# A decoder layer's two feed-forwards: the chunk pairs that take seven products, the engine that sums x, and the place of the raw weights

## The chip, the cores and the metric

The kernel runs on one core of one Trainium2 chip. The metric is the device time of one execution in microseconds (us); the lower the better. The core's engines run side by side, each through its own instructions in order: TensorE (PE in the profile; PEld is its loading of the stationary operand), VectorE (DVE), ScalarE (ACT), GpSimd (POOL) and SyncE (SP), which here does nothing but issue transfers. They wait for one another through semaphores.

## The reference, cut to what matters

One layer works on 256 tokens of width 2048 in float32: a feed-forward, a mixer (windowed attention beside an RWKV-7 recurrence), a cross-attention into 256 memory tokens, a second feed-forward, and a last norm. The change touches the two feed-forwards alone, whose inner width is 5632.

```python
def rms_norm(x, g):
    xf = x.astype(jnp.float32)
    y = xf * lax.rsqrt(jnp.mean(xf * xf, axis=-1, keepdims=True) + NORM_EPS)
    return (y * g.astype(jnp.float32)).astype(x.dtype)

def swiglu(h, w_gate, w_up, w_down):
    return (jax.nn.silu(h @ w_gate) * (h @ w_up)) @ w_down
...
x = x + 0.5 * swiglu(rms_norm(x, ffn1_norm[l]), ffn1_w_gate[l], ffn1_w_up[l], ffn1_w_down[l])
x = gated_parallel_mixer(...)
x = memory_cross_attention(...)
x = x + 0.5 * swiglu(rms_norm(x, ffn2_norm[l]), ffn2_w_gate[l], ffn2_w_up[l], ffn2_w_down[l])
return rms_norm(x, final_norm)
```

## The kernel before, in words

**Stages.** Three pools of on-chip memory follow one another: f1 holds the first feed-forward (0 to about 740 us in the profiled execution), mx the mixer and the cross-attention (to about 1570 us), f2 the second feed-forward (to the end). Pools f2 and mx use the same addresses; a tile of f2 waits for those tiles of mx that lay where it lies. At the end of the cross-attention GpSimd writes x to memory (x3d); in f2 `reload` (L1360, a transfer on GpSimd's queue for each of four column blocks) brings it back as the residual to which the feed-forward adds.

**Products.** A matmul of float32 is made of three of a rounded type (`times`, L397 to 399): with x = xhi + xlo and a weight = hi + lo, they are xhi by hi, xhi by lo, xlo by hi. Each handles 128 tokens, a chunk of 128 of the summed dimension, and 512 output columns.

**Weights.** A unit is two chunks by 512 columns of raw weights. SyncE loads them (`load`, L301 to 316) 4 items ahead, 8 in a feed-forward: there mostly two units together, in a tile raw2 (4 buffers) of the current pool, else one, in a tile raw (4 buffers). `split_unit` makes hi on ScalarE (L324) and lo = raw - hi on VectorE (L325), `AHEAD` = 2 units before TensorE wants them. `next_item` calls both.

**One feed-forward.** The 11 blocks of 512 inner columns go in `GROUPS` of 4, 4 and 3; after each group comes its part of the down product (L621 adds it to x). The first block of all makes gate and up by plain `product`, 12 matmuls a unit. Every other block makes both together in `product_pair`: eight chunk pairs q of two chunks each, as 2 x 2 blocks (two token halves by two chunks on one side, two chunks by gate and up on the other). In most pairs that is eight products of three matmuls, 24 in all. In the pairs of `SEVEN` it is seven products, p1 to p7, 21 matmuls, in the manner of Strassen and Winograd. They need sums of x's blocks and sums of the weights. The p-values lie in PSUM banks: p1, p3 and p5 in the three banks mm, p2 and p4 in acc (three banks), p6 and p7 in tr (two banks, which the transposes use as well). After the last pair of `SEVEN`, ScalarE copies p1 to the tile hb, and VectorE combines p5, p6, p7 and hb to the tiles u2, u3 (L499 to 501). The later pairs run plainly on p2 to p5. At the last of them (q = 7) VectorE adds the rest (L513, 516, 520), ScalarE applies Silu (L514, 517), and VectorE multiplies gate and up (L521) into hb.

**Sums of the weights** (`sums`, L328 to 344), for every block and every pair in `SEVEN`: four additions (L335 to 338) on VectorE, two casts to thi on ScalarE (L340), two tlo = sum - thi on VectorE (L341).

**Sums of x** (`combinations`, L409 to 446), once in a feed-forward. For each pair q up to the last in `SEVEN`, GpSimd adds xhi and xlo to one float32 tile (L423), and makes from it four sums (a pair in `SEVEN`, L429 to 432) or two differences (a pair before the last of `SEVEN` that is not in it: `EARLY`, L435). Then ScalarE casts them to chi (L438), and VectorE forms clo (L440). The tiles u between them have two buffers. In the code a pair's sums start once its x chunks are made (`x.done`).

**x and its norm.** `Norm.block` transposes x by blocks (`feat`), and ScalarE casts it to xhi (L560), VectorE makes xlo (L561), and ScalarE squares it for the norm (L569). After the fourth block `rstd` (L576 to 583) makes the scale r of each token: VectorE reduces the squares' sums, GpSimd takes the power -1/2 (L582). The scale is applied behind the gate and up products, so x goes unscaled into the matmuls. The Silu of the first block (L607) is the first that reads r.

**Transposes of hb.** `transposed` brings a finished block's hb to the layout of the down product: two `feat` (four transposes each into a bank tr, L534), each followed by `split` (a cast to hhi on ScalarE, L537; hlo on VectorE).

**Order.** Sums of x, transposes, reloads and the like are Python generators in groups (`Interleave`); the products call `tick`, and each tick lets every group go one step. The framework then orders each engine's instructions anew within what the data allow, and puts the semaphores.

Of the kernel before, what the change touches and what calls it, by code (L numbers as in the profile page):

```python
# [34 lines left out]
AHEAD, LOADED = 2, 4  # L35


SEVEN = (1, 3)
EARLY = tuple(q for q in range(max(SEVEN)) if q not in SEVEN)


# [87 lines left out]
def decoder_layer(ctx: ExitStack, tc: tile.TileContext, a: dict, out: bass.AP):  # L129
# [276 lines left out]
                k + i == 0, k + i == nk - 1,  # L406
            )

    def combinations(sp, x: Act):  # L409


        n = 4 * len(SEVEN) + 2 * len(EARLY)
        parts = [sp.tile([P, n, P], F32R, tag="c" + e, name="c" + e) for e in ("hi", "lo")]
        c = {"parts": parts, "at": {}, "done": False}

        def work():
            o = 0
            for q in range(max(SEVEN) + 1):
                while not {2 * q, 2 * q + 1} <= x.done:
                    yield  # L420
                v = sp.tile([P, 2, 2, P], F32, tag="u", name="u", bufs=2)
                f = sp.tile([P, 4, P], F32, tag="u", name="u", bufs=2)
                pool.tensor_tensor(  # L423
                    v[:].rearrange("p k t n -> p k (t n)"), f32(x.at(0, 2 * q, 2)),
                    f32(x.at(1, 2 * q, 2)), ALU.add,
                )
                if q in SEVEN:
                    n = 4
                    pool.tensor_tensor(f[:, 0], v[:, 0, 1], v[:, 1, 1], ALU.add)  # L429
                    pool.tensor_tensor(f[:, 1], f[:, 0], v[:, 0, 0], ALU.subtract)  # L430
                    pool.tensor_tensor(f[:, 2], v[:, 0, 0], v[:, 0, 1], ALU.subtract)
                    pool.tensor_tensor(f[:, 3], v[:, 1, 0], f[:, 1], ALU.subtract)
                else:
                    n = 2
                    pool.tensor_tensor(f[:, :2], v[:, :, 0], v[:, :, 1], ALU.subtract)  # L435
                yield from idle(3)
                s = slice(o, o + n)
                act.copy(parts[0][:, s], f[:, :n])  # L438
                dve.tensor_tensor(parts[1][:, s], f[:, :n], f32(parts[0][:, s]), ALU.subtract)
                c["at"][q] = o  # L440
                o += n
                yield
            c["done"] = True

        bg.spawn("mem", work())
        return c

    def product_pair(sp, x: Act, c, r, w):

        pw, _, nk, _, n = plan[at["product"]]
        assert pw[0].tensor is w.tensor
        at["product"] += 1
        b, begun = {}, set()
        hb = sp.tile([P, 2, 512], F32, tag="hb", name="hb", bufs=2)
        u2, u3 = (sp.tile([P, 512], F32, tag="u", name="u", bufs=2) for _ in range(2))
        late = nk // KU - 1  # L460

        def add(to, x_, w_, last):
            if to not in b:
                b[to] = {"p1": mm, "p3": mm, "p5": mm, "p2": acc, "p4": acc}.get(to, tr)()
            times(
                b[to][:], x_, w_, to not in begun, last, skip_group_check=True,
            )
            begun.add(to)

        def of_x(t, k):  # L470
            return [x.at(p, k)[:, t * P : (t + 1) * P] for p in range(2)]

        def of_c(q, i):
            return [p[:, c["at"][q] + i, :] for p in c["parts"]]

        def of_w(parts_, i):
            return [p[:, i, :] for p in parts_]

        for q in range(nk // KU):
            k = KU * q  # L480
            last = q == late
            if q in SEVEN:
                bg.until(lambda: c["done"])
                g, u, s = next_item()
                end = q == max(SEVEN)
                seven = (
                    ("p1", of_x(0, k), of_w(g, 0), end), ("p2", of_x(0, k + 1), of_w(g, 1), False),
                    ("p3", of_c(q, 3), of_w(u, 1), False), ("p5", of_c(q, 0), of_w(s, 0), end),
                    ("p7", of_c(q, 2), of_w(s, 1), end), ("p6", of_c(q, 1), of_w(s, 2), end),
                    ("p4", of_x(1, k + 1), of_w(s, 3), False),  # L490
                )
                for i, p in enumerate(seven):
                    add(*p)
                    if i % 2:
                        bg.tick()
                    if end and i == 1:
                        act.copy(hb[:, 0], b["p1"][:])
                if end:
                    dve.tensor_tensor(u2[:], b["p6"][:], hb[:, 0], ALU.add)  # L499
                    dve.tensor_tensor(u3[:], b["p7"][:], u2[:], ALU.add)  # L500
                    dve.tensor_tensor(u2[:], b["p5"][:], u2[:], ALU.add)
                continue
            g, u = next_item()
            for to, t, wt in (("p2", 0, g), ("p4", 1, g), ("p3", 0, u), ("p5", 1, u)):
                for i in range(KU):
                    off = to == "p3" and q in EARLY
                    add(
                        to, of_c(q, i) if off else of_x(t, k + i), of_w(wt, i),
                        last and i == KU - 1,
                    )  # L510
                if last:
                    if to == "p2":
                        dve.tensor_tensor(hb[:, 0], b["p2"][:], hb[:, 0], ALU.add)  # L513
                        act.activation(hb[:, 0], hb[:, 0], AF.Silu, scale=r[0])  # L514
                    elif to == "p4":
                        dve.tensor_tensor(hb[:, 1], b["p4"][:], u3[:], ALU.add)
                        act.activation(hb[:, 1], hb[:, 1], AF.Silu, scale=r[1])
                    else:
                        t, v = (0, u2) if to == "p3" else (1, u3)
                        dve.tensor_tensor(v[:], b[to][:], v[:], ALU.add)  # L520
                        dve.scalar_tensor_tensor(  # L521
                            hb[:, t], v[:], r[t], hb[:, t], ALU.mult, ALU.mult
                        )
                bg.tick()
        return hb
# [18 lines left out]
    class Norm:  # L544
        def __init__(self, gain, x=None):
            self.gain = gain
            self.ss = stat.tile([P, 2, 4], F32, tag="ss", name="ss")
            self.x = x or Act(
                [xtp.tile([P, KD, T], F32R, tag="xhi", name="xhi")],
                [xtp.tile([P, KD, T], F32R, tag="xlo", name="xlo")], KD,  # L550
            )
# [32 lines left out]


    def feed_forward(sp, x, norm: Norm, wg, wu, wd, done, begin_last=lambda: None, last=False):
        c = combinations(sp, norm.x)
        for gi, (j0, nj) in enumerate(GROUPS):
            h = Act(
                [sp.tile([P, 16, T], F32R, tag="hhi", name="hhi")],  # L590
                [sp.tile([P, 16, T], F32R, tag="hlo", name="hlo")], 16,
            )

            def transposed(hb, c):
                for q in range(2):
                    split(h, c + 2 * q, 2, feat(hb, [2 * q * P, (2 * q + 1) * P]))
                    yield

            for j in range(j0, j0 + nj):
                if j > 0:  # L600
                    hb = product_pair(sp, norm.x, c, norm.r, wg)
                    bg.spawn("feat", transposed(hb, 4 * (j - j0)))
                    continue
                pg = product(norm.x, wg)
                hb = sp.tile([P, 2, 512], F32, tag="hb", name="hb", bufs=2)
                for t in range(2):
                    act.activation(hb[:, t, :], pg[t][:], AF.Silu, scale=norm.r[t])  # L607
                pu = product(norm.x, wu)
                for t in range(2):
                    dve.scalar_tensor_tensor(  # L610
                        hb[:, t, :], pu[t][:], norm.r[t], hb[:, t, :], ALU.mult, ALU.mult
                    )
                bg.spawn("feat", transposed(hb, 4 * (j - j0)))
            if gi == len(GROUPS) - 1:
                begin_last()
            for n in range(4):
                end = gi == len(GROUPS) - 1
                pd = product(h, wd, skew=last and end and n == 3)
                for t in range(2):
                    xs = x[:, t, n * 512 : (n + 1) * 512]  # L620
                    dve.scalar_tensor_tensor(xs, pd[t][:], 0.5, xs, ALU.mult, ALU.add)  # L621
                if end:
                    done(n)
# [796 lines left out]
```

## Time and profile before

| | before |
|---|---|
| median of 3 runs | 2307.45 us (2306.52 to 2311.22) |
| the profiled execution, its own time | 2307.24 us |
| its span in the trace | 2305.5 us |
| TensorE matmul, busy | 2279.0 us, 10751 instructions |
| weight load, busy (overlaps the matmuls) | 1867.7 us |
| VectorE, busy | 1511.0 us, 1784 instructions |
| ScalarE, busy | 1143.8 us, 1534 instructions |
| GpSimd, busy | 159.1 us, 221 instructions |
| read from HBM | 417.56 MB |

A group in the profile reads "line, engine, operation, output<-inputs, partitions x elements, count", then times. A row of the timeline has the start, the duration, the engine, the line and operation, and in brackets how long the engine had stood idle before it and what ended that. A row of the waits has who waited, "<-" for whom, then total in us, count and longest. In the table of stretches each engine has its busy time and the number of its instructions; PEclk is the clock that TensorE was granted, as a share of full speed. Matmuls overlap: each has a duration, but the next one starts before it ends.

### The profile page before, as it was taken

To read this page: it belongs to the slowest core of one execution; us is meant where nothing else is said; L and a number is where in the kernel's file an instruction comes from. 1 tells how busy PE (TensorE), PEld (TensorE's weight loads), DVE (VectorE), ACT (ScalarE), POOL (GpSimd) and SP (SyncE) were. 2 spreads that over 40 slices of the span, in tenths; PEclk is the share of its full clock that TensorE was granted. 3 is DMA by queue.
4 is the path that set the end of the run, shared out by engine and by line. 5 is a ranking of instruction groups with operands and counts; after the bars stand their busy time and mean duration, and the time that the engine had idled before them with its cause. 6 is when DMAs were issued, how large, how long until landed. Compare 5 with 4: busy or idle time off the path is not lost.

```text
span 2305.5 us, 27706 instructions
## 1 busy us (share of the span) xinstructions
PE 2279.0 (99%) x10751; PEld 1867.7 (81%) x10751; DVE 1511.0 (66%) x1784; ACT 1143.8 (50%) x1534; POOL 159.1 (7%) x221
## 2 busy tenths in 40 slices
PE   9999999999999999999999999998999999999998
PEld 7888888888888877778888888887888888888886
DVE  6875677657865477895444466556875677756865
ACT  6544445434545467444344446555554454534544
POOL 4000000000000000201220030003000000000001
PEclk9999999999999999999999999999999999999999
DMA  7555565565564544676423576647565565555553
GB/s 252 188 200 190 193 201 194 190 199 192 201 233 143 163 139 138 193 227 210 141 85 101 166 262 224 191 164 245 183 207 195 183 205 197 197 187 201 200 201 128
DMA packets 219236, 432.73 MB, mean 188 GB/s; under 512 B 14139, under 2 KB 16416, under 8 KB 219104
## 3 DMA queue, kind: packets, MB, share of 16 engines
q1 hardware_dynamic: 210432, 404.78, 52.7%
q0 software_dynamic: 8208, 25.39, 3.4%
q8 instruction: 84, 1.38, 0.2%
q10 hardware_dynamic: 464, 0.79, 0.1%
q14 instruction: 48, 0.39, 0.0%
HBM read 417.56 MB, written 13.11 MB: 187 GB/s over the span
## 4 chain that ended last, share of the span: by engine, by line
PE 90%; issue 4%; DVE 2%; ACT 1%; DMA 1%; POOL 1%; SPq 0%; POOLq 0%; ACTq 0%; DVEq 0%
PE acc L397 21%; PE acc L398 21%; PE acc L399 21%; PE mm L399 6%; PE mm L397 6%; PE mm L398 6%; PE tr L534 2%; PE mm L1119 1%; PE tr L399 1%; PE tr L397 1%; PE tr L398 1%; DVE lo L325 1%; PE tr L1088 1%; ACT s L762 0%; ACT hi L324 0%
## 5 line engine op out<-in xcount | busy, mean ns | idle before, releaser
L325 DVE TENSOR_TENSOR lo<-raw,hi 128x1024 fp32r<-128x1024 f32 (+1 forms) x770 | 918.3, 1198 | 652.3 <-ACT hi L324 648.4
L324 ACT CAST hi<-raw 128x1024 fp32r<-128x1024 f32 (+1 forms) x770 | 784.4, 1025 | 930.1 <-PE acc L399 713.5
L397 PE MATMUL acc<-hi,xhi 128*128 128x512 f32 (+1 forms) x1256 | 500.1, 399 | 7.8 <-ACT hi L324 2.9
L398 PE MATMUL acc<-lo,xhi 128*128 128x512 f32 (+1 forms) x1256 | 491.6, 391 | 3.5 <-DVE lo L325 3.4
L399 PE MATMUL acc<-hi,xlo 128*128 128x512 f32 (+1 forms) x1256 | 490.3, 391 | 1.2 <-DVE xlo L561 1.2
L397 PEld LDWEIGHTS acc<-hi,xhi 128*128 128x128 f32 x1256 | 236.5, 188 | 60.6 <-issue 5.1
L398 PEld LDWEIGHTS acc<-lo,xhi 128*128 128x128 f32 x1256 | 237.0, 189 | 53.7 <-DVE lo L325 5.5
L399 PEld LDWEIGHTS acc<-hi,xlo 128*128 128x128 f32 x1256 | 236.5, 188 | 50.3 <-DVE xlo L561 2.5
L397 PE MATMUL acc<-hi,hhi 128*128 128x512 f32 x704 | 275.0, 391 | 0.0
L399 PE MATMUL acc<-hi,hlo 128*128 128x512 f32 x704 | 274.6, 390 | 0.0
L398 PE MATMUL acc<-lo,hhi 128*128 128x512 f32 x704 | 274.6, 390 | 0.0
L398 PE MATMUL mm<-lo,xhi 128*128 128x512 f32 x440 | 171.2, 389 | 0.0
L399 PE MATMUL mm<-hi,xlo 128*128 128x512 f32 x440 | 171.2, 389 | 0.0
L397 PE MATMUL mm<-hi,xhi 128*128 128x512 f32 x440 | 171.2, 389 | 0.0
L398 PEld LDWEIGHTS acc<-lo,hhi 128*128 128x128 f32 x704 | 132.2, 188 | 27.1
L399 PEld LDWEIGHTS acc<-hi,hlo 128*128 128x128 f32 x704 | 132.2, 188 | 26.9
L397 PEld LDWEIGHTS acc<-hi,hhi 128*128 128x128 f32 x704 | 132.2, 188 | 26.8
L341 DVE TENSOR_TENSOR tlo<-raw,thi 128x1024 fp32r<-128x1024 f32 x80 | 95.9, 1219 | 19.9 <-ACT thi L340 19.9
L398 PEld LDWEIGHTS mm<-lo,xhi 128*128 128x128 f32 x440 | 82.6, 188 | 17.3
L397 PEld LDWEIGHTS mm<-hi,xhi 128*128 128x128 f32 x440 | 82.6, 188 | 17.2
L399 PEld LDWEIGHTS mm<-hi,xlo 128*128 128x128 f32 x440 | 82.6, 188 | 17.2
L340 ACT CAST thi<-raw 128x1024 fp32r<-128x1024 f32 x80 | 82.0, 1050 | 28.1 <-PE acc L399 27.9
(347 smaller groups left out, 2618.2 us busy)
## 6 DMA issues: line engine op xcount, KB each, us to landing
raw<-in_ffn_w_up_dram SPq DMA_DIRECT2D x88, 1024.0 KB, 5.1
raw<-in_ffn_w_down_dram SPq DMA_DIRECT2D x88, 1024.0 KB, 5.1
raw<-in_ffn_w_gate_dram SPq DMA_DIRECT2D x84, 1024.0 KB, 5.1
raw<-in_w_in_dram SPq DMA_DIRECT2D x136, 512.0 KB, 3.5
raw<-in_w_out_dram SPq DMA_DIRECT2D x32, 512.0 KB, 4.7
raw<-in_w_proj_attn_dram SPq DMA_DIRECT2D x16, 512.0 KB, 3.5
raw<-in_w_proj_rwkv_dram SPq DMA_DIRECT2D x16, 512.0 KB, 6.4
raw<-in_w_cross_kv_dram SPq DMA_DIRECT2D x16, 512.0 KB, 3.6
```

Of the source, the lines that this page charges most:

```text
L324: act.copy(hi[:, s], raw[:, s])
L325: dve.tensor_tensor(lo[:, s], raw[:, s], f32(hi[:, s]), ALU.subtract)
L340: act.copy(hi[:, 2 * i : 2 * i + 2], t[:])
L341: dve.tensor_tensor(lo[:, 2 * i : 2 * i + 2], t[:], f32(hi[:, 2 * i : 2 * i + 2]), ALU.subtract)
L397: pe.matmul(o, xh, hi, start=first, stop=False, **how)
L398: pe.matmul(o, xh, lo, start=False, stop=False, **how)
L399: pe.matmul(o, xl, hi, start=False, stop=last, **how)
L534: pe.transpose(b[:, o : o + P], tok[:, t, col : col + P], ident[:])
L1088: pe.matmul(b[e][:, m * P : (m + 1) * P], x1[r, j, cs_], x2[r, j, cs_], start=True, stop=True,)
L1119: pe.matmul(vb[:, o : o + P][:, r], lhs(e), rhs[:, r], start=first and e == 0, stop=True, **ek,)
```

## The change

- `SEVEN` goes from pairs 1 and 3 to pairs 0 and 2, and `EARLY` with it from 0 and 2 to 1: the sums of x are made for three pairs, not four. The number of matmuls stays.
- The sums of x are formed by VectorE in place of GpSimd. In the code they start only when the norm's scale r is known (`Norm.r`, None at first), and there is one step of the generator, not three, before the cast, and one behind it.
- Within a pair of `SEVEN` the order p1 p2 p3 p5 p7 p6 p4 becomes p1 p2 p7 p6 p4 p3 p5.
- A finished block's transposes are no longer queued at once: they are held in c["next"] and queued after the combination (L499 to 501 before) of the next block. Those of a group's last block are queued at once, as are those of the block j = 0.
- In the second feed-forward one buffer each of hhi, hlo, thi, tlo and two of hb are allocated first and not used, so that they take the first addresses of the pool, and raw2 lies behind them.

```diff
-SEVEN = (1, 3)
+SEVEN = (0, 2)
...
-    def combinations(sp, x: Act):
+    def combinations(sp, norm):
...
-        n = 4 * len(SEVEN) + 2 * len(EARLY)
+        x, n = norm.x, 4 * len(SEVEN) + 2 * len(EARLY)
...
-        c = {"parts": parts, "at": {}, "done": False}
+        c = {"parts": parts, "at": {}, "done": False, "next": []}
 
         def work():
             o = 0
+            while norm.r is None:
+                yield
             for q in range(max(SEVEN) + 1):
-                while not {2 * q, 2 * q + 1} <= x.done:
-                    yield
                 v = sp.tile([P, 2, 2, P], F32, tag="u", name="u", bufs=2)
                 f = sp.tile([P, 4, P], F32, tag="u", name="u", bufs=2)
-                pool.tensor_tensor(
+                dve.tensor_tensor(
                     v[:].rearrange("p k t n -> p k (t n)"), f32(x.at(0, 2 * q, 2)),
                     f32(x.at(1, 2 * q, 2)), ALU.add,
                 )
                 if q in SEVEN:
                     n = 4
-                    pool.tensor_tensor(f[:, 0], v[:, 0, 1], v[:, 1, 1], ALU.add)
+                    dve.tensor_tensor(f[:, 0], v[:, 0, 1], v[:, 1, 1], ALU.add)
...
                 else:
                     n = 2
-                    pool.tensor_tensor(f[:, :2], v[:, :, 0], v[:, :, 1], ALU.subtract)
-                yield from idle(3)
+                    dve.tensor_tensor(f[:, :2], v[:, :, 0], v[:, :, 1], ALU.subtract)
+                yield
                 s = slice(o, o + n)
                 act.copy(parts[0][:, s], f[:, :n])
+                yield
                 dve.tensor_tensor(parts[1][:, s], f[:, :n], f32(parts[0][:, s]), ALU.subtract)
...
                     ("p1", of_x(0, k), of_w(g, 0), end), ("p2", of_x(0, k + 1), of_w(g, 1), False),
-                    ("p3", of_c(q, 3), of_w(u, 1), False), ("p5", of_c(q, 0), of_w(s, 0), end),
                     ("p7", of_c(q, 2), of_w(s, 1), end), ("p6", of_c(q, 1), of_w(s, 2), end),
                     ("p4", of_x(1, k + 1), of_w(s, 3), False),
+                    ("p3", of_c(q, 3), of_w(u, 1), False), ("p5", of_c(q, 0), of_w(s, 0), end),
...
                     dve.tensor_tensor(u2[:], b["p5"][:], u2[:], ALU.add)
+                    while c["next"]:
+                        bg.spawn("feat", c["next"].pop())
...
     def feed_forward(sp, x, norm: Norm, wg, wu, wd, done, begin_last=lambda: None, last=False):
-        c = combinations(sp, norm.x)
+        if last:
+            for tag, shape, dt, bufs in (
+                ("hhi", [P, 16, T], F32R, 1), ("hlo", [P, 16, T], F32R, 1),
+                ("hb", [P, 2, 512], F32, 2), ("thi", [P, 4, 512], F32R, 1),
+                ("tlo", [P, 4, 512], F32R, 1),
+            ):
+                sp.tile(shape, dt, tag=tag, name=tag, bufs=bufs)
+        c = combinations(sp, norm)
...
-                    bg.spawn("feat", transposed(hb, 4 * (j - j0)))
+
+                    c["next"].append(transposed(hb, 4 * (j - j0)))
+                    if j == j0 + nj - 1:
+                        bg.spawn("feat", c["next"].pop())
```

More of the change, by code (lines that the diff above doesn't have):

```diff
@@ L428, in work @@
                     n = 4
-                    pool.tensor_tensor(f[:, 0], v[:, 0, 1], v[:, 1, 1], ALU.add)
-                    pool.tensor_tensor(f[:, 1], f[:, 0], v[:, 0, 0], ALU.subtract)
-                    pool.tensor_tensor(f[:, 2], v[:, 0, 0], v[:, 0, 1], ALU.subtract)
-                    pool.tensor_tensor(f[:, 3], v[:, 1, 0], f[:, 1], ALU.subtract)
+                    dve.tensor_tensor(f[:, 0], v[:, 0, 1], v[:, 1, 1], ALU.add)
+                    dve.tensor_tensor(f[:, 1], f[:, 0], v[:, 0, 0], ALU.subtract)
+                    dve.tensor_tensor(f[:, 2], v[:, 0, 0], v[:, 0, 1], ALU.subtract)
+                    dve.tensor_tensor(f[:, 3], v[:, 1, 0], f[:, 1], ALU.subtract)
                 else:
                     n = 2
-                    pool.tensor_tensor(f[:, :2], v[:, :, 0], v[:, :, 1], ALU.subtract)
-                yield from idle(3)
+                    dve.tensor_tensor(f[:, :2], v[:, :, 0], v[:, :, 1], ALU.subtract)
+                yield
                 s = slice(o, o + n)
                 act.copy(parts[0][:, s], f[:, :n])
+                yield
                 dve.tensor_tensor(parts[1][:, s], f[:, :n], f32(parts[0][:, s]), ALU.subtract)
@@ L546, in __init__ @@
             self.gain = gain
+            self.r = None
             self.ss = stat.tile([P, 2, 4], F32, tag="ss", name="ss")
```

## The prediction, made before the changed kernel had been run

> **What bounds the kernel now.** I read the busy time by stage first, because the page's 99% for TensorE is an average. The columns after the stretch are its length, then TensorE matmul, weight load, VectorE, ScalarE and GpSimd busy time with instruction counts, the granted TensorE clock, and the DMA share.
>
> ```profile
> core 0 of [0], span 2305.5 us
> core 0: us, PE busy (x) PEld busy (x) DVE busy (x) ACT busy (x) POOL busy (x), PEclk, DMA share, GB/s
> 0.00:36.00 36.00, 30.98 (x143) 24.29 (x144) 22.40 (x35) 24.66 (x51) 25.59 (x56) 1.00 0.79 277
> ...
> 80.00:740.00 660.00, 660.00 (x2964) 544.28 (x2964) 456.00 (x500) 316.88 (x357) 3.13 (x6) 1.00 0.58 194
> ...
> 1582.00:1608.00 26.00, 20.16 (x73) 15.44 (x73) 15.32 (x12) 12.28 (x15) 15.54 (x17) 0.87 0.71 250
> 1608.00:2296.00 688.00, 688.00 (x3076) 567.49 (x3075) 475.19 (x513) 326.67 (x359) 11.64 (x11) 1.00 0.56 190
> ```
>
> From 80 to 740 us (the first feed-forward) and from 1608 to 2296 us (the second) TensorE is busy for every microsecond, at full clock. The change neither adds nor removes a matmul: it takes the seven products (21 matmuls in place of 24) in two of eight chunk pairs, as before. In those 1348 us nothing can be won, and something can be lost. What can be won lies at the starts of the two feed-forwards: 5.0 us idle in the first 36, and 5.8 us idle in the 26 from 1582 on, where the mean clock is 0.87 besides. So I asked what TensorE waits for there; first 1582 to 1608, then 0 to 36. Each row gives total, count and longest.
>
> ```profile
> PE acc L397 <- ACT hb L607: 2.5, 1, 2.5
> PE acc L397 <- ACT hi L324: 2.1, 1, 2.1
> PE acc L398 <- DVE lo L325: 1.3, 1, 1.3
> ```
> ```profile
> PE acc L399 <- DVE xlo L561: 1.2, 2, 0.9
> ...
> PE tr L534 <- DVE xlo L561: 0.3, 1, 0.3
> ```
>
> All three waits of the first list go back to the sums of x on GpSimd. ScalarE works in order, and it copies each finished sum (chi) before it goes on to the weights (hi):
>
> ```profile
> 1578.86 0.19 ACT L569 ACTIVATION_READ_ACCUMULATOR junk<-x 128x1 f32 x1
> 1583.33 0.40 ACT L438 CAST chi<-u 128x256 fp32r<-128x256 f32 x1 [4.28 <-POOL u L435]
> 1583.64 1.99 ACT L324 CAST hi<-raw 128x1024 fp32r<-128x1024 f32 x2
> ```
> ```profile
> 1581.79 0.75 POOL L1360 DMA_DIRECT2D x<-x3d  x1 [1.55 <-issue]
> 1582.56 0.73 POOL L435 TENSOR_TENSOR u<-u 128x256 f32<-128x256 f32 x1
> ```
>
> ScalarE stands for 4.28 us in front of a copy whose sum GpSimd forms only after it has issued the reload of x. The cast of the fifth weight unit is queued behind that copy, and its matmuls start late:
>
> ```profile
> 1584.73 0.73 PE L397 MATMUL acc<-hi,xhi 128*128 128x512 f32 x2 [2.06 <-ACT hi L324]
> 1586.75 0.80 PE L398 MATMUL acc<-lo,xhi 128*128 128x512 f32 x1 [1.29 <-DVE lo L325]
> ```
>
> The last sum does it once more. It delays a weight cast, the Silu table behind the cast, the Silu, and the matmul that wants the Silu's PSUM bank:
>
> ```profile
> 1599.01 0.62 ACT L438 CAST chi<-u 128x512 fp32r<-128x512 f32 x1 [3.98 <-POOL u L432]
> 1599.54 1.04 ACT L324 CAST hi<-raw 128x1024 fp32r<-128x1024 f32 x1
> 1600.60 1.28 ACT L607 ACT_TABLE_LOAD   x1
> 1601.90 1.27 ACT L607 ACTIVATE hb<-acc,rs 128x512 f32<-128x512 f32 x2
> ```
> ```profile
> 1599.30 0.39 PE L397 MATMUL acc<-hi,xhi 128*128 128x512 f32 x1
> 1599.53 0.39 PE L398 MATMUL acc<-lo,xhi 128*128 128x512 f32 x1
> 1599.75 0.39 PE L399 MATMUL acc<-hi,xlo 128*128 128x512 f32 x1
> 1602.64 0.50 PE L397 MATMUL acc<-hi,xhi 128*128 128x512 f32 x1 [2.49 <-ACT hb L607]
> ```
>
> Matmuls start 0.225 us apart (1599.30 to 1599.75 in two) but last 0.39, so a wait costs about 0.165 us more than its row says: 2.49 stands for 2.66.
>
> At the start of the kernel the sums hurt in another way. These are VectorE's rows, then GpSimd's:
>
> ```profile
> 4.22 0.29 DVE L211 TENSOR_TENSOR center<-ident,bdmean 128x128 f32<-128x128 f32 x1 [4.22 <-POOL bdmean L208]
> ...
> 13.84 2.41 DVE L325 TENSOR_TENSOR lo<-raw,hi 128x1024 fp32r<-128x1024 f32 x1
> 16.18 0.86 DVE L561 SCALAR_TENSOR_TENSOR xlo<-tr,g_ffn,xhi 128x256 fp32r<-128x256 f32 x2
> ```
> ```profile
> 13.86 1.30 POOL L423 TENSOR_TENSOR u<-xhi,xlo 128x512 f32<-128x512 f32 x1
> ```
>
> One weight split takes 2.41 us while GpSimd reads x; the same form takes 1.22 below. The xlo behind it is what TensorE waits for.
>
> **The change part by part.** *Sums on VectorE, start of the kernel.* 28 GpSimd additions go in both feed-forwards; 24 come to VectorE, and each has one pair of chi and clo fewer. Without the GpSimd read the 13.84 split ends some 1.2 us sooner, and the matmul can then start as soon as the one before it allows: 0.9 + 0.165 = 1.06 us. The two other waits (1.2 - 0.9 = 0.3, and 0.3) are each 0.47 with the same addition. Together 2.0 us. Against it, VectorE takes in this stage three adds of 512 columns, eight of 128 and one of 256: 3 x 0.6 + 8 x 0.25 + 0.4 = 4.2 us, minus a clo. Its order in the built program puts them between the xlo of the later blocks, not after them: the norm's scale, which the Python code waits for, is known to the tracer, and the scheduler moves the adds up. They fit into VectorE's idle time there (36 - 22.4 = 13.6 us up to 36). If they delayed the two smaller waits and as much again, the gain would be 0; the highest is 2.0. I take 1.9.
>
> *Sums on VectorE, second feed-forward.* In the new order ScalarE has two chi copies ahead of the fifth unit's cast, and VectorE sums for them at once, when x's squares are done at 1579.05. Step by step: a small reduction 0.2 (estimate), the 512-column add 0.69, three dependent 128-column adds and one between them 3 x 0.29 + 0.2, giving 1581.0; chi 0.62 plus hand-over, 1581.65; clo 0.69, then the next sum 0.5, 1582.9; chi 0.40, 1583.3; cast 1.05, 1584.4. The matmul started at 1584.73, so 0.3 is won. The lo half then stands behind the third sum on VectorE: about 1585.05 + 1.22 = 1586.3 against 1586.75, so 0.45 is won, and the first two waits largely stay; VectorE has taken GpSimd's place in them. But the whole series ends at about 1588 and no copy is left ahead of the later cast. The table load and first Silu then run 1.28 + 0.7 after the first PSUM bank is complete, inside the 12 matmuls (12 x 0.225 = 2.7 us) until the bank is needed. The 2.66 us go. So does the half clock behind them: 0.13 x 26 us = 3.4 us of clock are missing in that stretch, in two episodes, and one of these, about 1.6 us, goes. Sum: 0.45 + 2.66 + 1.6 = 4.7. Lowest: neither goes, 0. Highest: the first clock episode goes too, 6.3.
>
> By the Trainium skill, TensorE: Matmul & The Clock Gate, "HAM oscillation", TensorE should keep its clock if no idle gap exceeds about 3.4 us. By that the 2.66 us gap would not cost the 1.6, and the time would be 1.6 us higher than mine. The 0.87 in a stretch whose longest wait is 2.5 us disagrees, and I follow the row.
>
> *Raw weights behind the other tiles (second feed-forward only).* Their addresses overlap tiles that were done long before, so the first of these loads need not wait for the last product of the cross-attention. That cast was behind chi, not behind a load: 0. What covers it is ScalarE's order; with that gone it would be worth at most the 2.06 us of its wait. Earlier loads share queues with the write of x3d, which only the reload waits for; the scale, now behind the first reload on GpSimd, is wanted at 1597, 14 us later.
>
> *Seven products in pairs 0 and 2.* The first sums of weights in a pair must now be ready at its start instead of one chunk pair later. The trace already makes them in the pair before, from 1699.91; the adds issue 0.6 us apart, the splits 1.14:
>
> ```profile
> 1699.91 0.69 DVE L335 TENSOR_TENSOR raw<-raw,raw 128x512 f32<-128x512 f32 x1
> 1700.51 0.68 DVE L336 TENSOR_TENSOR raw<-raw 128x512 f32<-128x512 f32 x1
> ...
> 1704.59 1.22 DVE L325 TENSOR_TENSOR lo<-raw,hi 128x1024 fp32r<-128x1024 f32 x1
> 1705.73 1.22 DVE L341 TENSOR_TENSOR tlo<-raw,thi 128x1024 fp32r<-128x1024 f32 x1
> ```
>
> The narrow place is the second set. Counted from the pair's first matmul, VectorE has in order: the last PSUM add (from 0.2) 0.6, an add 0.6, a gating product 0.7, two splits 2.28, two adds 1.2, a split 1.14, an add 0.6, two tlo 2.28: done at 9.6. It is wanted after 21 + 24 + 6 = 51 matmuls, 11.5. So 1.9 us to spare, 20 times. Cost 0; without that cover every 0.1 us over costs 2.
>
> *Transposes held back, order p1 p2 p7 p6 p4 p3 p5.* They move from the first chunk pair to the fourth (8 x about 0.11 us either way) and leave both transpose banks to p6 and p7. In the first pair of a feed-forward the old rule stays, and its second half waits for the VectorE read of p6: by the same counting some 0.2 us each, 0.4 in all; 0 to 2.
>
> **The rivals.** *The sums fall late in every pair (slower).* Place: tlo of the third chunk pair, TensorE's queue stopped at p7. It decides once that VectorE series takes over 11.5 us instead of 9.6; at 1 us over it costs 20 us and gives 2307.24 - 6.2 + 20 = 2321. For it: VectorE is packed there and works in order. Against it: all its terms are measured and TensorE waits nowhere in such series now. *The waits of the second feed-forward keep their length, with VectorE for GpSimd.* For it: that is what I find for the first two. Against it: the third needs a late last sum. Only the start wins: 2307.24 - 1.9 + 0.4 = 2305.7. *VectorE's adds cost at the start what the freed read gave.* Then 2307.24 - 4.7 + 0.4 = 2302.9, and 2305 if they cost 2 more. For it: they do stand between xlo, not "later" as the change says.
>
> **How the numbers follow.** The profiled execution took 2307.24 us (1.74 beside its span), 0.2 under the median 2307.45. 2307.24 - 1.9 - 4.7 + 0.4 = 2301.0. Chances: this forecast 0.62, its own range 2298.4 (start 2.0, second stage 6.3, cost 0 give 2298.9, and a little for the spread of runs) to 2304; second feed-forward unchanged 0.14; start eaten up 0.11; late sums 0.13. A measurement tells 0.2% (4.6 us) from no change, so faster means below 2302.8, and slower above 2312.1. The forecast lies mostly below the first bound, the two middle cases mostly between: faster 0.61, same 0.26, slower 0.13. The range 2298.4 to 2310 leaves out most of the late sums and a little below.
>
> **What would show it.** Right: the 13.84 split near 1.2 us; one clock episode instead of two after 1582, with waits near 1.9 and 1.3 us in place and no wait for the Silu; no TensorE wait between 80 and 740 or in the last 688 us, and about 28 GpSimd instructions fewer. Wrong: TensorE waits for tlo or thi, 20 times alike; waits for xlo before 36 us that are longer than now; a Silu wait of over 2 us still there.

## The result and the profile after

| | median | runs | range | ratio to before |
|---|---|---|---|---|
| before | 2307.65 us | 10 | 2306.52 to 2312.53 | |
| changed | 2301.98 us | 10 | 2298.71 to 2305.99 | 0.997 (95%: 0.996 to 0.9979) |

The change takes 5.7 us off, 0.25%; the forecast was 2301.0. The profiled execution of the changed kernel happens to be the longest of its ten (2305.99 us, span 2304.2), only 1.25 us under the profiled one of before (2307.24). So the two spans say little, and the stages must be read one by one. Line numbers are those of each kernel: L534, L560, L561, L607 and L521 of before are L537, L564, L565, L621 and L524 of the changed one. The busy time by stage of the changed kernel, columns as before:

```profile
core 0 of [0], span 2304.2 us
...
0.00:36.00 36.00, 33.40 (x152) 27.22 (x153) 24.48 (x46) 26.18 (x52) 12.07 (x42) 0.95 0.84 295
...
80.00:740.00 660.00, 660.00 (x2966) 545.74 (x2965) 456.02 (x500) 319.91 (x360) 3.85 (x7) 1.00 0.57 194
...
1582.00:1608.00 26.00, 23.37 (x96) 18.54 (x95) 14.48 (x19) 13.57 (x15) 2.14 (x3) 0.93 0.70 239
1608.00:2296.00 688.00, 685.66 (x3057) 565.77 (x3055) 475.21 (x513) 327.12 (x358) 11.64 (x11) 1.00 0.54 188
```

In 1582 to 1608 TensorE now makes 96 matmuls for 73, and its mean clock is 0.93 for 0.87: one half-clock stretch in place of two. In the first 36 us it makes 152 for 143, though the clock, 1.00 before, is 0.95 there. New is the last row: in the second feed-forward TensorE now misses 2.3 of 688 us (688 - 685.66). Whom it waits for from 1560 us on, and in the first 80:

```profile
PE acc L398 <- DVE lo L325: 3.2, 2, 2.1
PE acc L397 <- ACT hi L324: 1.5, 1, 1.5
```
```profile
PE acc L397 <- ACT xhi L564: 1.5, 1, 1.5
PE mm L174 <- POOL ones L170: 1.1, 1, 1.1
```

GpSimd makes 193 instructions for 221, 28 fewer. Against before, the wait for the Silu (2.5 us) is gone, and all three waits for xlo; the waits for hi and lo at 1582 us stay, shorter. But one of the two waits for lo, of 2.1 us, is not at 1584 us. It stands in the last block (rows of TensorE, then of VectorE):

```profile
2186.96 0.39 PE L397 MATMUL acc<-hi,xhi 128*128 128x512 f32 x1
2189.41 0.50 PE L398 MATMUL acc<-lo,xhi 128*128 128x512 f32 x1 [2.06 <-DVE lo L325]
...
2190.50 0.63 PE L398 MATMUL acc<-lo,xhi 128*128 128x512 f32 x1
2190.93 0.63 PE L399 MATMUL acc<-hi,xlo 128*128 128x512 f32 x1
```
```profile
2186.86 0.69 DVE L335 TENSOR_TENSOR raw<-raw,raw 128x512 f32<-128x512 f32 x1 [3.68 <-DMA raw<-in_ffn_w_up_dram]
2187.47 0.74 DVE L524 SCALAR_TENSOR_TENSOR hb<-u,rs,hb 128x512 f32<-128x512 f32 x1
2188.13 2.35 DVE L325 TENSOR_TENSOR lo<-raw,hi 128x1024 fp32r<-128x1024 f32 x2
```

VectorE stands 3.68 us in front of the first weight sum of the third chunk pair, whose up weights have not landed. Behind it in order are the lo of the pair that TensorE is working on. After the wait the matmuls start 0.43 us apart (2190.50 to 2190.93) in place of 0.23: half clock, for some 3 us. The loads of that time (line, queue, count, KB each, median us from issue to landing) show the neighbour, the final norm's gain:

```profile
raw<-in_ffn_w_gate_dram SPq DMA_DIRECT2D x2, 1024.0 KB, 5.0
raw<-in_final_norm_dram POOLq DMA_DIRECT2D x4, 256.0 KB, 6.8
raw<-in_ffn_w_up_dram SPq DMA_DIRECT2D x1, 1024.0 KB, 9.8
```

An up load takes 9.8 us where the gate loads around it take 5.0. GpSimd issues the gain's four loads in the middle of it, at 2176.1 to 2178.9 us.

### The profile page after: what moved, and what is told of

The parts are those of the page before. It is cut to its first block, busy times and chain, and to the rows that moved or that the text cites. A ratio compares the mean times of both kernels' runs of the same rounds, so it can differ in the third digit from the quotient of the medians.

```text
span 2304.2 us, 27723 instructions
## 1 busy us (share of the span) xinstructions
PE 2281.5 (99%) x10751; PEld 1873.4 (81%) x10751; DVE 1514.8 (66%) x1806; ACT 1146.6 (50%) x1532; POOL 131.8 (6%) x193
## 4 chain that ended last, share of the span: by engine, by line
PE 89%; issue 4%; DVE 3%; DMA 2%; ACT 1%; POOL 0%; SPq 0%; POOLq 0%; ACTq 0%; DVEq 0%
PE acc L397 20%; PE acc L398 20%; PE acc L399 20%; PE mm L398 6%; PE mm L399 6%; PE mm L397 6%; PE tr L537 2%; DVE lo L325 1%; PE mm L1133 1%; PE tr L398 1%; PE tr L1102 1%; PE tr L399 1%; PE tr L397 1%; DMA raw<-in_ffn_w_up_dram 1%; ACT hi L324 0%
## 5 line engine op out<-in xcount | busy, mean ns | idle before, releaser
L397 PE MATMUL mm<-hi,xhi 128*128 128x512 f32 x480 | 188.0, 392 | 0.0
L399 PE MATMUL mm<-hi,xlo 128*128 128x512 f32 x480 | 187.0, 390 | 0.0
L398 PE MATMUL mm<-lo,xhi 128*128 128x512 f32 x480 | 187.0, 390 | 0.0
L399 PEld LDWEIGHTS mm<-hi,xlo 128*128 128x128 f32 x480 | 90.1, 188 | 18.8
L397 PEld LDWEIGHTS mm<-hi,xhi 128*128 128x128 f32 x480 | 90.2, 188 | 18.4
L398 PEld LDWEIGHTS mm<-lo,xhi 128*128 128x128 f32 x480 | 90.1, 188 | 18.4
```

The lines of the kernel that those rows point to most:

```text
L397: pe.matmul(o, xh, hi, start=first, stop=False, **how)
L398: pe.matmul(o, xh, lo, start=False, stop=False, **how)
L399: pe.matmul(o, xl, hi, start=False, stop=last, **how)
```

## The experiments

The program makes 10751 matmul instructions in every version, so the versions can be laid side by side by the time from one numbered matmul's start to another's. The table is worked out that way from the traces; the mixer's column (from 718 us, shortly before the mixer begins, to about 1497) holds work that no version changes, and it scatters by itself by up to 5.6 us (777.3 to 783.0). Each row is one profile. "clock" says after which waits the matmuls of a feed-forward started 0.43 us apart for some 3 us.

| version | start (1st to 151st) | first pairs (to 401st) | rest of first feed-forward (to 3201st) | mixer (to 7201st) | start of second (to 7901st) | last block (10151st to 10451st) | clock | span |
|---|---|---|---|---|---|---|---|---|
| before | 36.72 | 55.87 | 624.77 | 778.38 | 161.80 | 67.20 | 1586, 1603 | 2305.5 |
| changed | 34.50 | 56.47 | 624.36 | 780.22 | 157.23 | 70.81 | 9, 1586, 2190 | 2304.2 |
| again | 34.76 | 56.51 | 624.33 | 777.93 | 155.99 | 68.98 | 9 | 2299.1 |
| sums_only | 34.33 | 55.89 | 624.77 | 780.44 | 157.14 | 67.20 | 1586 | 2300.5 |
| sums_pool | 35.81 | 56.45 | 624.33 | 779.34 | 158.71 | 70.92 | 1588, 2192 | 2306.2 |
| gain_later | 34.69 | 56.60 | 624.34 | 777.34 | 155.71 | 68.73 | none | 2298.0 |
| no_place | 34.57 | 56.43 | 624.35 | 778.52 | 157.17 | 70.70 | 1585, 2188 | 2302.4 |
| sums_late | 34.54 | 56.85 | 624.37 | 779.18 | 152.70 | 68.39 | none | 2296.7 |
| gain_sync | 34.78 | 56.45 | 624.34 | 777.70 | 155.82 | 66.83 | 8 | 2296.3 |
| both_late | 34.66 | 56.84 | 624.34 | 778.28 | 152.93 | 66.85 | 9 | 2294.3 |
| both_again | 34.52 | 56.96 | 624.33 | 782.96 | 153.38 | 66.84 | none | 2299.4 |
| late_13 | 34.26 | 55.87 | 624.79 | 779.73 | 152.29 | 67.21 | none | 2294.8 |

**again: the changed kernel, a second profile.** No edit.

> The changed kernel once more, for a second profile. In its first profile TensorE stood 2.2 us (start to start) at 2187 us, where VectorE waited 3.68 us for an up-weight load that took 9.82 us beside the loads of the final norm's gain, and the clock was at half for about 3.4 us behind it. Theory (built into the change: the first chunk pair's sums are now wanted a pair earlier): the wait at about 2187 is there again, 1.5 to 3 us, and the waits at 1582 and 1584 are again near 1.5 and 1.1 us. Rival (an accident of that run): no wait beyond 1600 us.

Measured: one run of 2300.81 us. The late load is there again; the wait behind it is 1.8 us, and this time the clock held. The first two waits at the start of the second feed-forward are 1.49 and 1.14 us, to the hundredth as in the first profile, and yet here they draw no half clock. The same stretch of this second profile:

```profile
1582.00:1608.00 26.00, 24.86 (x108) 20.29 (x109) 16.12 (x19) 14.17 (x15) 0.00 (x0) 1.00 0.70 237
```

So the late load belongs to the change, and the half clock behind a wait comes or not from run to run (the last section shows what differs).

**sums_only: the sums of x on VectorE, nothing else of the change.** `combinations` as changed, in the kernel before:

```diff
-                pool.tensor_tensor(
+                dve.tensor_tensor(
...
+            while norm.r is None:
+                yield
...
-SEVEN = (0, 2)
+SEVEN = (1, 3)
```

(the last two lines against the changed kernel).

> The kernel before, with the sums of x on VectorE as the change has them and nothing else of it (pairs 1 and 3, old order of products, transposes at once, old places). Theory (the gain is the sums' alone: 2.2 us at the start, 4.6 at the start of the second feed-forward; the pairs only cost): about 2300.5, no wait near 2187 us. Rival (placement or pairs bring the gain): 2306 to 2307.

Measured: 2302.38 us in 10 runs against 2308.48 in 26, ratio 0.9973 (0.9964 to 0.9982). That is the whole of the change's gain by one of its five parts. This part holds the engine and the new steps and start of the generator together; they were not tried apart. Start and second start are those of the changed kernel, and the last block has the 67.20 us of before. The size was 1.9 us off (2302.38 for 2300.5).

**sums_pool: the sums of x back on GpSimd, all else as changed.**

```diff
-                dve.tensor_tensor(
+                pool.tensor_tensor(
```

(for all of them, with the old waits and steps of the generator).

> The changed kernel with the sums of x back on GpSimd, with the old waits and steps; all else as changed. Theory: the waits for chi at 1583 and 1599 come back (2 and 2.5 us on TensorE, with two half-clock stretches), the start takes some 2 us more, the wait at 2187 stays: 2308 to 2311, slower than before by 1 to 3 us. Rival (the gain is not the sums'): about 2302, as the changed kernel.

Measured: 2307.72 us in 11 runs, ratio 0.9993 (0.9984 to 1.0002): the time of before, and 0.3 us under the low end expected. Two parts of the expectation missed: the start takes 1.1 to 1.3 us more than in the changed kernel (35.81 for 34.50 to 34.76), not 2, and the wait for the Silu did not come back. ScalarE's rows of this version:

```profile
1588.03 0.41 ACT L438 CAST chi<-u 128x256 fp32r<-128x256 f32 x1 [1.73 <-POOL u L435]
...
1593.36 0.62 ACT L438 CAST chi<-u 128x512 fp32r<-128x512 f32 x1 [3.97 <-POOL u L432]
1593.88 2.00 ACT L324 CAST hi<-raw 128x1024 fp32r<-128x1024 f32 x2
...
1599.46 1.27 ACT L620 ACTIVATE hb<-acc,rs 128x512 f32<-128x512 f32 x2
```

The last chi still waits 3.97 us for GpSimd, but it is done at 1594 us, not 1599.6: pairs 0 and 2 need sums for three pairs, pairs 1 and 3 for four, and in the kernel before the third of the four chi stands at 1593.67 us, as early as the last one here. Either part alone takes the Silu wait away; the shorter waits before it only VectorE shortens (sums_pool has 2.58 us in front of the fifth unit's hi, the changed kernel 1.49).

**gain_later.** The gain's tiles were to come from other buffers:

```diff
+                if n == 0:
+                    for _ in range(2):
+                        wp.tile([P, KU, 512], F32, tag="raw", name="raw", bufs=4)
```

> The changed kernel with the final norm's gain loaded into the buffers of the other weight sums, so that these loads start some 15 us later, behind the last block's second sums. Theory: the up load before 2187 us takes 5 to 6 us, TensorE waits nowhere beyond 1600 us, and 2.2 to 4 us are won against the changed kernel: 2298 to 2300. Rival (the late load is an accident, or has another cause than the gain's loads): about 2302, the wait as before.

Measured: 2303.95 us in 11 runs, ratio 0.9979 (0.997 to 0.9987), and the edit did nothing that shows: the gain's loads stayed behind the same tlo (issued at 2172.0 to 2174.8 us, the last block being some 4 us earlier as a whole). So the two tiles that nobody uses did not push them back, and the run is the changed kernel a third time: it leaves open whether the gain's loads are to blame. Its up load took 9.31 us by the trace, and the wait is there, at 1.6 us.

**no_place: without the tiles allocated first in the second feed-forward.**

```diff
-        if last:
-            for tag, shape, dt, bufs in (
...
-                sp.tile(shape, dt, tag=tag, name=tag, bufs=bufs)
```

> The changed kernel without the tiles that are allocated first in the second feed-forward, so that the raw weights lie where they lay before. Theory (the cast of the fifth unit waits behind chi, not for its load): the first raw2 loads start some us later, the waits at 1582 and 1584 us stay near 1.5 and 1.1 us, time as the changed kernel within 1 us. Rival (the earlier loads are what shortened the wait at 1582): that wait grows by 0.5 to 2 us, and its releaser is a cast that itself waited for a load; 1 to 3 us slower than the changed kernel.

Measured: 2302.59 us in 8 runs, ratio 0.9972 (0.9962 to 0.9982), beside 0.997 with the tiles; the start of the second feed-forward takes 157.17 us for 157.23. The edit does move the loads: the first of the up weights is issued at 1569.98 us, with the tiles at 1564.90. The place is worth nothing here all the same, since the cast waits behind chi:

```profile
1580.89 0.41 ACT L438 CAST chi<-u 128x256 fp32r<-128x256 f32 x1 [1.22 <-DVE u L435]
1581.20 1.99 ACT L324 CAST hi<-raw 128x1024 fp32r<-128x1024 f32 x2
```

**sums_late: chi behind the first Silu.** An order on ScalarE alone; the additions stay on VectorE.

```diff
-            while norm.r is None:
+            while "go" not in c:
...
-                act.copy(parts[0][:, s], f[:, :n])
+                with tc.issue_after(c["go"].ins): act.copy(parts[0][:, s], f[:, :n])
...
-                    act.activation(hb[:, t, :], pg[t][:], AF.Silu, scale=norm.r[t])
+                    c["go"] = act.activation(hb[:, t, :], pg[t][:], AF.Silu, scale=norm.r[t])
```

> The changed kernel with every chi copy on ScalarE ordered behind the Silu of the block j = 0, in both feed-forwards; the additions themselves stay on VectorE. Theory (what is left of the waits at 1582 and 1584 us is chi ahead of the cast on ScalarE, and sums ahead of lo on VectorE): the first of the two waits goes, the second falls under 0.9 us, the stretch from 1582 keeps its clock; 2 to 4 us faster than the changed kernel, 9 to 10 faster than before. Rival (the cast is bound by its load, or the copies then run late and delay the weight sums of the block j = 1): the waits stay, or new ones of 1 to 2 us stand at the start of that block; no gain.

Measured: 2298.64 us in 5 runs against 2309.38 in 12, 10.7 us under before, ratio 0.9958 (0.9944 to 0.9971). The two casts of the next weight units now run as soon as x's squares are done, and so do the splits:

```profile
1578.14 2.11 ACT L324 CAST hi<-raw 128x1024 fp32r<-128x1024 f32 x2
...
1592.81 1.26 ACT L621 ACTIVATE hb<-acc,rs 128x512 f32<-128x512 f32 x2
1593.96 1.04 ACT L324 CAST hi<-raw 128x1024 fp32r<-128x1024 f32 x1
1594.90 0.62 ACT L438 CAST chi<-u 128x512 fp32r<-128x512 f32 x1
```

Beyond 1560 us TensorE waits only for the late load (1.2 us). The stage takes 152.7 us, 3.0 us under the 155.7 of the changed kernel where its clock held, and 4.5 under 157.2 where it did not. The expected second wait of up to 0.9 us is not there. At the first pairs 0.3 to 0.4 us are lost (56.85 for 56.47 to 56.60).

**gain_sync: the gain's loads on SyncE's queue.**

```diff
-                pool.dma_start(fin(n), a["final_norm"][cb].unsqueeze(0).broadcast_to([P, 512]))
+                nc.sync.dma_start(fin(n), a["final_norm"][cb].unsqueeze(0).broadcast_to([P, 512]))
```

On that queue they stand behind two more weight loads, which wait for buffers.

> The changed kernel with the final norm's gain loaded by SyncE's queue, behind the up load that the last block's third pair wants, in place of GpSimd's queue. Theory (that up load takes 9.3 to 9.9 us only because it shares the engines with the gain's loads): it lands in 5 to 6 us, TensorE waits nowhere beyond 1600 us, and 1.5 to 3.6 us are won against the changed kernel. Rival (the up load is slow for another reason): the wait at about 2185 us stays, no gain.

Measured: 2300.17 us in 5 runs, ratio 0.9959 (0.9946 to 0.9971). The transfers of that time:

```profile
raw<-in_ffn_w_gate_dram SPq DMA_DIRECT2D x2, 1024.0 KB, 5.0
raw<-in_ffn_w_up_dram SPq DMA_DIRECT2D x2, 1024.0 KB, 5.9
raw<-in_final_norm_dram SPq DMA_DIRECT2D x4, 256.0 KB, 7.9
```

The up load that took 9.8 us lands in 5.0 (the 5.9 is the median with the next one, which takes 6.7; in the changed kernel, with no gain beside it, that one took 7.5). TensorE waits for no load beyond 1600 us, and the last block takes 66.83 us, 1.9 to 4.0 us less than with the late load.

**both_late: both edits.**

> Both edits at once: chi behind the first Silu, and the final norm's gain on SyncE's queue. Theory: the two gains add, 4 to 7 us faster than the changed kernel and 10 to 13 faster than before, and the runs scatter less, since fewer waits can draw a half-clock stretch. Rival: one of the two waits only hid the other, and both together bring no more than the better one.

Measured: 2295.99 us in 5 runs, ratio 0.9946 (0.9933 to 0.9958): 13.4 us under before, and the fastest version. The two gains add: 152.93 and 66.85 us in their stages. Whether the runs scatter less cannot be told: these five spread over 4.1 us, those of gain_sync over 4.1 and those of sums_late over 1.5. This is all that TensorE waits for from 1560 us to the end:

```profile
PE tr L537 <- DVE hb L624: 0.2, 1, 0.2
```

**both_again and late_13.** The same version once more, and beside it one with pairs 1 and 3, the old order of products, transposes at once and old places: the kernel before, with the sums on VectorE and chi behind the Silu.

> The version with both edits (chi behind the first Silu, the gain on SyncE's queue) once more, beside the one with pairs 1 and 3. Theory: 0.994 to 0.995 of before again, no wait of TensorE over 0.5 us between 36 and 740 us or beyond 1560 us. Rival: a new wait that the first profile happened not to show.

> The kernel before with the sums of x on VectorE and chi behind the first Silu, but with pairs 1 and 3, the old order of products, transposes at once, old places, and the final norm's gain on GpSimd's queue. Theory (pairs 0 and 2 are worth nothing by themselves: 0.6 us lost in the first block and 0.4 won in the rest of the first feed-forward, and a late load in the last block that pairs 1 and 3 do not feel): as fast as the version with both edits within 1.5 us. Rival (pairs 0 and 2 save something that the late load has hidden): 2 us or more slower than the version with both edits.

Measured: 2299.13 us, ratio 0.9956 (0.9942 to 0.997), and 2300.82 us, ratio 0.996 (0.9948 to 0.9973), 5 runs each against 2308.81 in 9. The intervals overlap nearly whole: pairs 0 and 2 are worth nothing that these runs can tell, at most a microsecond or two. Even the sign is open: late_13 is 1.7 us slower by the medians, where at most 1.5 was expected, and by the profiles, without the mixer's column, 0.9 and 1.3 us faster. The first version came out at 0.9956 for the 0.994 to 0.995 expected, with an interval that takes in the 0.9946 of both_late; in its profile the mixer took 783.0 us for 778.3, the widest scatter seen. Its waits for hb, in front of transposes, were 0.4 us between 36 and 740 and 0.7 beyond 1560, the second over the 0.5 expected:

```profile
PE tr L537 <- DVE hb L624: 0.7, 1, 0.7
```

## Why the prediction was right, and where not

**The time.** 2301.0 forecast, 2301.98 measured, direction and size right. The cause named, the sums of x on VectorE, is enough for it: sums_only, with this part alone, has the whole gain. That sums_pool, with all parts but this one, has none is a balance: its profile wins 0.9 us at the start and 3.1 in the second start (161.80 to 158.71), and loses 3.7 in the last block. So one part of the gain, the Silu wait, has two causes, and either is enough.

**Start of the kernel (1.9 us).** Measured 2.0 to 2.2 (36.72 against 34.50 to 34.76), of which sums_pool keeps 0.9. VectorE's rows of the changed kernel, at the place of the 2.41 us split:

```profile
13.86 1.23 DVE L325 TENSOR_TENSOR lo<-raw,hi 128x1024 fp32r<-128x1024 f32 x1
15.00 0.87 DVE L565 SCALAR_TENSOR_TENSOR xlo<-tr,g_ffn,xhi 128x256 fp32r<-128x256 f32 x2
15.79 0.68 DVE L423 TENSOR_TENSOR u<-xhi,xlo 128x512 f32<-128x512 f32 x1
```

1.23 us as forecast, and the additions in between delay nobody. With GpSimd back (sums_pool) the same split takes 2.18 us; VectorE's row, then GpSimd's:

```profile
13.95 2.18 DVE L325 TENSOR_TENSOR lo<-raw,hi 128x1024 fp32r<-128x1024 f32 x1
```
```profile
13.73 1.31 POOL L423 TENSOR_TENSOR u<-xhi,xlo 128x512 f32<-128x512 f32 x1
```

In both kernels the slow split ends 1.09 us behind GpSimd's add (16.25 behind 15.16, 16.13 behind 15.04), so nearly its whole work comes after it.

The Trainium skill, SBUF — State Buffer, "SBUF: two separate sides", says that VectorE with two on-chip inputs and a GpSimd operation that reads on-chip memory lock each other out for a whole instruction; the three durations (2.41, 2.18, 1.23) and these two ends agree. What was not foreseen is a half-clock stretch at 9 us in two of the three profiles of the changed program (changed, again and gain_later); it costs nothing that shows, for the third, without it, takes 34.69 us.

**Second feed-forward (4.7 us).** Measured 4.6 where the clock fell once (161.80 to 157.23) and 5.8 to 6.1 where it held. The working can be checked row by row:

```profile
1580.72 0.62 ACT L438 CAST chi<-u 128x512 fp32r<-128x512 f32 x1 [1.88 <-DVE u L432]
1582.56 0.40 ACT L438 CAST chi<-u 128x256 fp32r<-128x256 f32 x1 [1.22 <-DVE u L435]
1582.87 1.99 ACT L324 CAST hi<-raw 128x1024 fp32r<-128x1024 f32 x2
...
1596.83 1.28 ACT L621 ACT_TABLE_LOAD   x1 [0.35 <-PE acc L399]
1598.12 1.27 ACT L621 ACTIVATE hb<-acc,rs 128x512 f32<-128x512 f32 x2
```

First sums done 1580.72 (1581.0 in the working), second chi 1582.56 (1582.9), the two matmuls at 1583.97 and 1585.84 (1584.4 and 1586.3). The second of them thus came 0.9 us sooner than before, 0.2 of it because the whole stage began sooner (1496.8 to 1496.6 at the 7201st matmul): some 0.7 us for the 0.45 of the sum. So VectorE did take GpSimd's place in the first two waits, and the third went. One reason was too narrow: I gave the Silu wait's end to VectorE, and sums_pool shows that three pairs in place of four end it too.

**Raw weights behind the other tiles (0).** Right, and shown by no_place. late_13, where chi is out of the way too, has the old places and takes 152.29 us in that stage, the shortest of all: there they cost nothing that shows either.

**Seven products in pairs 0 and 2 (0).** This step failed. The narrow place named, tlo of the third pair after 11.5 us, holds: in 19 of the 20 blocks that have such pairs TensorE waits nowhere there. What I left out of the series is that its first term needs a load. "Without that cover every 0.1 us over costs 2" was put for work on VectorE; what went over was the landing of the up weights, in one block. In the kernel before the same load, the third last of the up weights, was as slow beside the gain's, 9.6 us by the trace (7.6 is the median with the next one), and TensorE waits for nothing there:

```profile
raw<-in_ffn_w_up_dram SPq DMA_DIRECT2D x2, 1024.0 KB, 7.6
raw<-in_final_norm_dram POOLq DMA_DIRECT2D x4, 256.0 KB, 6.4
```

The sums were then wanted a pair later. The price is 1.5 to 3.7 us (68.73 to 70.92 for 67.20), by whether the clock falls as well. That the gain's loads are what slows the up load, gain_sync shows: without them it takes 5.0 us, and the wait is gone.

**Transposes held back and the new order (0.4).** In the first pairs the loss was 0.6 us (55.87 to 56.47); the 0.4 won in the rest of the first feed-forward (624.77 to 624.36) was not foreseen. Which of the parts moved together (pairs, order, transposes) makes which of the two was not tried.

Summed up as measured: 2.0 to 2.2 won at the start, 4.6 to 6.1 at the second, 0.2 lost net for the pairs, 1.5 to 3.7 for the late load, so 2.7 to 6.6 us; the median moved by 5.7. The forecast had 6.2. So far as these profiles show, two errors stood against each other in it: it counted one half-clock stretch in the second start as sure, and three of six profiles with those waits have none; and it missed the late load. That it came within 1 us of the median is in part luck. The kernel before has one profile only, so how often its own two stretches come is open too; among runs with a mean clock of 0.997 it takes 2306.5 to 2307.6 us (7 of the 26 runs beside sums_only) and the changed kernel 2302.3 and 2303.6, some 4 us less.

## What to carry to other kernels

On an engine that works in order, look at what a small copy waits for before asking what the large one behind it waits for: here a 0.4 us cast that nobody wanted for some 40 us held up the weights, and ordering it behind a later instruction won 3.0 us in its stage that were still lost after its producer had moved to another engine. When a step is moved ahead, its transfers' landing times belong in the slack as well as the arithmetic, and the slack has to be checked at the place where an unrelated transfer is slowest. And when versions differ by a few us, lay the traces side by side by numbered instruction: one stage that nobody touched (the mixer) scatters by 5.6 us, as much as the whole change gains.

## What the hardware showed unexpectedly

The granted clock falls behind short waits, and the same waits draw it in one run and not in another. The pair at 1582 us (1.4 to 1.5 and 1.1 to 1.4 us) drew half clock in the changed kernel's first profile, in no_place and in sums_only, and none in again, gain_later and gain_sync. The records of the clock show what differs. In each of the nine profiles with more than one change, all of them lie on a grid with a step of 3.413 us, and the grid does not lie alike in all runs. Here are three cells of the grid (columns as before, the clock third from the end) about the pair of waits, in the changed kernel's first profile, then in again:

```profile
1578.86:1582.27 3.41, 3.41 (x16) 2.64 (x15) 3.29 (x10) 0.62 (x1) 2.15 (x3) 1.00 0.58 207
1582.27:1585.68 3.41, 0.94 (x3) 0.30 (x2) 3.31 (x8) 3.12 (x5) 1.87 (x3) 1.00 0.76 267
1585.68:1589.10 3.42, 3.26 (x8) 2.59 (x9) 2.97 (x4) 0.65 (x1) 0.00 (x0) 0.50 0.96 332
```
```profile
1578.40:1581.81 3.41, 2.09 (x10) 1.40 (x8) 3.26 (x7) 1.85 (x3) 3.14 (x5) 1.00 0.57 178
1581.81:1585.22 3.41, 2.10 (x8) 1.45 (x9) 3.38 (x7) 2.54 (x4) 0.00 (x0) 1.00 0.85 290
1585.22:1588.63 3.41, 3.41 (x17) 2.81 (x16) 2.54 (x3) 1.05 (x1) 0.00 (x0) 1.00 0.88 318
```

In the first both waits lie in one cell, which is idle for 2.47 us (3.41 - 0.94), and the next cell runs at half clock; in the second an edge of the grid parts them (1.32 and 1.31 us idle), and the clock holds. Between 1560 us and the last matmuls all twelve profiles agree: each of the nine cells in which TensorE is idle for 1.98 us or more is followed by one at half clock, and none of the others, idle for up to 1.85. That is no rule for other stretches: at the start and in the mixer the clock also fell behind some cells with 0.9 to 1.7 us idle, and behind others like them it did not. A stretch lasts 3.4 us by the records of the clock, six to eight matmuls that start 0.43 us apart in place of 0.23, and so costs 1.2 to 1.6 us; the ten runs of the changed kernel, with mean clocks from 0.995 to 0.999, spread over 7.3 us. The Trainium skill, TensorE: Matmul & The Clock Gate, "HAM oscillation", wants no idle gap over about 3.4 us; by these rows that is not enough, since no wait between matmuls behind which the clock fell was longer than 2.6 us (sums_pool, 1583 us). The same page says, under "What's actually happening", that the window in which activity is counted runs free of the kernel, and that the number of slow matmuls differs from run to run; the grid, which does not lie alike in all runs, agrees with that.
